# Rebuilding the entry of a feed-forward stage: operand tiles one by one, first weights ahead, two rooms for scaled rows

## The chip, the cores and the metric

The kernel runs on one core of a Trainium2 chip. The metric is the device time of one execution in microseconds (us), the median of several runs. One profiled execution of the kernel before is read beside them.

## What is computed

The program is one residual block on 1024 tokens of width 1024: a mixing stage (retention and forgetting attention), a cross attention, and a gated feed-forward. The change touches the entry of the last one:

```python
# reference, cut; h is (1, 1024, 1024), w_gate and w_up (1024, 2816), w_down (2816, 1024)
h = h + memory_cross_attention(rmsnorm(h, g_xattn), mem, ...)    # ends with  o @ w_xo
hn = rmsnorm(h, g_ffn)
h = h + (jax.nn.silu(hn @ w_gate) * (hn @ w_up)) @ w_down
```

All values are float32. Every matmul operand is cut in two parts (`hi`, a rounded copy made by ScalarE, and `lo`, the rest, made by VectorE), and a product of operands is three matmuls: hi·hi, hi·lo and lo·hi.

## The kernel before

**Stages.** `whole` (L1414) runs the mixing stage, `kv_main`, `wout_main`, `xattn_main`, `xo_main`, `hidden_main` and `down_main` in this order. The token rows go in eight tiles of 128 rows (t = 0 to 7), the 2816 hidden units in 22 blocks of 128 (f).

**Who sets the order.** Only TensorE's order is written out by hand. The stages are generators; the planner `Driver` (L93 on) takes a step of the first thread in its list that is ready, and otherwise a step of the main line. A step yields its estimated TensorE time in ns and a delay, which is stretched by `slow` (1.8 here). `take_tp` (L148 with `HOLD` 1.5) holds back transposes while both rooms of the PSUM tag `tp` are counted as taken. The orders of ScalarE, VectorE, GpSimd and SyncE come from the framework's list scheduler, which follows the program's order where nothing speaks against it. Every engine then runs its own queue strictly in order, and an instruction whose wait isn't over holds up all that stands behind it.

**Memory.** A tile belongs to a tag of a pool and the tag has `bufs` rooms. `raws` (L191) has three rooms of 4 KB under the tag `raw`. `wA` (L210) has five pairs `whi`, `wlo`, `big` (L213) eight rooms `b0` to `b7`, and `mx` (L860) the rooms `b8` to `b11`, `xs` (one row tile) and `gbc` (a broadcast gain). These three pools carry the weights and rows of the projection `w_xo` and belong to the stack `LW`. On the other side lie the residual rows `h` (stack `HP`, four tiles of two row tiles each) and `xr` (stack `R12`). Where a pool is closed and another opened on its bytes, a tile waits only for the users of older tiles on its own bytes.

**The way into the feed-forward.** `xo_main` (L1093) runs `out_proj` (L826): for each row tile two products of 24 matmuls with `w_xo`, VectorE adds them to `h[t]` (L838), and `f_norm(t)` (L1100) is spawned. `f_norm` waits until the row tile before it is done (`f_done`), scales the row into the single room `xs` (`norm`, L307 on: ScalarE squares at L310, a short chain of small operations, VectorE multiplies at L312), stores `h[t]` to DRAM, and after a delay transposes it on TensorE (L175) into `xr`. For t of 4 and more VectorE then makes four combinations of the quarters (L1125 to L1128). The 2x2 product of the tokens' two halves of rows and two halves of columns runs as seven block products (P1, P2, Q5, P6, P7, Q3, Q4), each of 12 matmuls per f.

`hidden_main` (L1174) begins as soon as four row tiles are done: for the first `AHEAD` = 3 blocks f it runs P1 and P2, whose weights (`load_gate`, L1155) are loaded through `raws` and lie in `b0` to `b5`. Then, with all eight row tiles done, `LW` is closed, a pool `ffn_x` is opened for the other five operands, and ScalarE and VectorE cut all five in two parts, first the columns 0 to 383 of all five, then 384 to 511 (L1250, L1251). After that `weights_of` (L1272) makes the weights of the products (sums `t13`, `t2`, `t4` of the four loaded blocks, then hi and lo), in the order Q5(0), P6(0), Q3(0), P7(0), Q5(1), Q4(0), ... `down_main` (L1307) follows.

Of the kernel before, what the change touches and what calls it, by code (L numbers as in the profile page):

```python
# [19 lines left out]
P = 128  # L20
D = 1024
T = 1024
NT = T // P
# [130 lines left out]
def trace(tc, a, out):  # L154
    nc = tc.nc
    ctx = ExitStack()
    drv = Driver()
# [51 lines left out]
    LW = ExitStack()  # L209
# [668 lines left out]
    def fox_end():  # L878
        yield lambda: fox_left[0] == 0 and hn_free[0] == NT
        FX.close()  # L880
        hp = pool("h", 1, side="right", stack=HP)
        pairs = [hp.tile([P, 2, D], F32, name=f"h{t}") for t in range(NT // 2)]
        st["h"] = [pairs[t // 2][:, t % 2] for t in range(NT)]
        st["h01"] = pairs[0].rearrange("p a (b c) -> p (a b) c", c=512)

    def kv_main():
# [206 lines left out]
    def xo_main():  # L1093
        w = st.pop("w_xo")
        h = st["h"]
        gff = gbc("gff")
        bcast(gff, a["g_ffn"])
        f_done = st["f_done"] = [0]

        def f_norm(t):  # L1100
            yield lambda: f_done[0] >= t
            xs = xs_tile("xs")
            norm(h[t], gff, xs)
            pol.dma_start(h_dram[t], h[t])
            yield 0.0, 4500.0
            cols = slice((t % 4) * P, (t % 4 + 1) * P)
            yield lambda: "xr" in st
            for b in range(2):
                yield from take_tp(2200)
                tp = ps_tp()  # L1110
                for j in range(4):
                    flip(tp[:, j, :], xs[:, (4 * b + j) * P:(4 * b + j + 1) * P])
                with prio(P_TP):
                    act.copy(st["xr"][t // 4][:, 4 * b:4 * b + 4, cols], tp)
                    if t < 4:
                        hi, lo = st["x1"][b][:, :4, cols], st["x1"][b][:, 4:, cols]
# [12 lines left out]
            f_done[0] += 1  # L1129
            yield 0.0, 2000.0  # L1130

        def opened():

            yield lambda: all(n == NX for n in o2_done)
            XA.close()
            xrp = pool("xr", 1, side="right", stack=R12)
            st["x1"] = [half(i, [P, 8, 512], "x1") for i in range(2)]
            st["xr"] = [xrp.tile([P, KC, 512], F32, name=f"xr{i}") for i in range(2)]

        drv.spawn(opened())  # L1140
        yield from out_proj(*st.pop("nxt_o2"), w, lambda t: None, lambda t: drv.spawn(f_norm(t)), first_gates)


# [16 lines left out]
    def first_gates():  # L1160
        st["gates"] = [load_gate(f) for f in range(AHEAD)]

    def into(q, terms, first):

        n = len(terms)
        for k, (wh, wl, xh, xl) in enumerate(terms):
            mm.matmul(q, wh, xh, start=first and k == 0, stop=False, skip_group_check=True)  # L1167
            mm.matmul(q, wh, xl, start=False, stop=False, skip_group_check=True)  # L1168
            mm.matmul(q, wl, xh, start=False, stop=k == n - 1, skip_group_check=True)  # L1169
            yield 700.0, 0.0  # L1170

    W1, RR = ExitStack(), ExitStack()

    def hidden_main():  # L1174

        f_done = st["f_done"]
        x1, xr = st["x1"], st["xr"]
        A = {"P1": (x1[0][:, :4], x1[0][:, 4:]), "P2": (x1[1][:, :4], x1[1][:, 4:])}
        alpha, beta, gamma, p1, s1, u2, q5, at = ({} for _ in range(8))
        pp, wp = [None], [None]  # L1180

        def row(f):
            if f not in at:
                at[f] = pp[0].tile([P, T], F32, name="at", tag="at")
            return at[f]

        def step(f, what, w):

            xh, xl = A[what]
            terms = [(w[0][:, k], w[1][:, k], xh[:, k], xl[:, k]) for k in range(4)]  # L1190
            if what == "P1":
                alpha[f] = ps_s()
                yield from into(alpha[f], terms, True)
                ab = raws.tile([P, 2, 512], F32, name="p1", tag="raw") if f < AHEAD else pp[0].tile([P, 2, 512], F32, name="p1", tag="p1")
                p1[f], s1[f] = ab[:, 0, :], ab[:, 1, :]
                act.copy(p1[f], alpha[f])
            elif what == "P2":
# [5 lines left out]
            elif what == "Q5":  # L1203
                gamma[f] = ps_tp().rearrange("p a b -> p (a b)")
                yield from into(gamma[f], terms, True)
                q5[f] = pp[0].tile([P, 512], F32, name="q5", tag="q5")
                act.copy(q5[f], gamma[f])
                if f < AHEAD:
                    act.activation(s1[f], s1[f], AF.Silu)
            elif what == "P6":  # L1210
                yield from into(alpha[f], terms, False)
                u2[f] = pp[0].tile([P, 512], F32, name="u2", tag="u2")
                act.copy(u2[f], alpha[f])
            elif what == "P7":
                yield from into(alpha[f], terms, False)
                c = row(f)
                dve.tensor_tensor(c[:, 512:], q5.pop(f), alpha[f], ALU.subtract)
            elif what == "Q3":
                yield from into(gamma[f], terms, False)
                c = row(f)  # L1220
                dve.tensor_tensor(c[:, :512], gamma.pop(f), u2.pop(f), ALU.subtract)
                dve.tensor_tensor(c[:, :512], c[:, :512], s1.pop(f), ALU.mult)
            else:
                yield from into(alpha[f], terms, False)
                s2 = pp[0].tile([P, 512], F32, name="s2", tag="s2")
                act.activation(s2, alpha.pop(f), AF.Silu)
                c = at.pop(f)
                dve.tensor_tensor(c[:, 512:], c[:, 512:], s2, ALU.mult)
                for g, hs in enumerate(GROUPS):
                    for i, fs in enumerate(hs):  # L1230
                        if f in fs:
                            pol.dma_start(a_dram[g][i][fs.index(f)], c)


        yield lambda: f_done[0] >= 4
        for f in range(AHEAD):
            gh, gl = st["gates"][f]
            yield from step(f, "P1", (gh[:, :4], gl[:, :4]))
            yield from step(f, "P2", (gh[:, 4:], gl[:, 4:]))

        yield lambda: f_done[0] == NT
        LW.close()
        wp[0] = pool("ffn_x", 1, stack=W1)
        xs = {"Q5": st["h01"], "P6": xr[0][:, :4], "P7": xr[1][:, :4], "Q3": xr[0][:, 4:], "Q4": xr[1][:, 4:]}
        for what, x in xs.items():
            A[what] = [wp[0].tile([P, 4, 512], F32R, name=f"x{what}{i}") for i in range(2)]
        for cols in (slice(0, 384), slice(384, 512)):
            for what, x in xs.items():
                hi, lo = (y[:, :, cols] for y in A[what])
                act.copy(hi, x[:, :, cols])  # L1250
                dve.tensor_tensor(lo, x[:, :, cols], f32(hi), ALU.subtract)  # L1251
        R12.close()
        HP.close()
        ra = pool("ffn_a", 1, side="right", stack=RR)
        rr = pool("ffn_w", 1, side="right", stack=RR)
        pp[0] = pool("ffn_t", 1, stack=W1)
# [4 lines left out]
        seq.insert(0, (0, "Q5"))  # L1261
        for f in range(AHEAD, NF_):
            seq += [(f, p) for p in ("P1", "Q5", "P6", "P2", "P7", "Q3", "Q4") if (f, p) not in seq]
        raw, t13, t2 = {}, {}, {}

        def load_w(f):

            raw[f] = r = ra.tile([P, 4, 4, P], F32, name="raw_w", tag="raw_w", bufs=2)
            for b, (src, k) in enumerate((("w_gate", 0), ("w_up", 0), ("w_up", 1), ("w_gate", 1))):
                sp.dma_start(r[:, b], a[src][k * 512:(k + 1) * 512, f * P:(f + 1) * P].rearrange("(k p) c -> p k c", p=P))  # L1270

        def weights_of(f, what):  # L1272
            r = raw[f]
            if what == "Q5":
                t13[f] = ra.tile([P, 2, 4, P], F32, name="t13", tag="t13", bufs=1)
# [17 lines left out]
                load_w(f + 2)  # L1293
            return hi, lo

        load_w(0)
        load_w(1)
        made = []
        for n, (f, what) in enumerate(seq):
            while len(made) < min(n + RING - 2, len(seq)):  # L1300
# [6 lines left out]
    def down_main():  # L1307
        h = {}
        RR.close()
        W1.close()  # L1310
        halves_stack.close()
        dl = pool("down_l", 1)
        dr = [pool(f"down_r{i}", 1, side="right") for i in range(2)]
# [139 lines left out]
```

## Time and profile before

| | us |
|---|---|
| median of 3 runs (1605.29 to 1613.33) | 1608.91 |
| the profiled execution, as timed | 1609.22 |
| its span in the trace | 1607.5 |

TensorE (PE) is busy for 1552.7 us of the span, VectorE (DVE) for 995.0, ScalarE (ACT) for 751.8, GpSimd (POOL) for 155.2. PE is the matrix engine's matmul queue, SP the queue of SyncE, which here only issues DMAs. A row of a timeline gives start and duration in us, engine, line, operation, output and inputs, and in brackets the idle time before it with what ended that. Matmuls overlap: a row of 0.39 us follows its predecessor after 0.23 us.

### The profile page before, as it was taken

Reading aid. Unit: us, or ns where it says so; the run is one execution under the profiler, and the core shown is the slowest. Engines: PE = TensorE matmul, PEld = TensorE weight load, DVE = VectorE, ACT = ScalarE, POOL = GpSimd, SP = SyncE. Lnnn points to the kernel's source line nnn. Section 1 sums busy time; section 2 is a strip of 40 time slices with the busy share of each in tenths; the row PEclk is TensorE's granted clock in tenths of the full one; section 3 lists DMA queues with packets and bytes.
Section 4 is the critical chain, followed back from the end, with each engine's and each line's share of the span. In section 5 each row is a group of like instructions: output and inputs, shape, how many; then the busy total and the mean of one; then the engine's idle time right before and its main releaser. Section 6 shows DMA issues by size and latency. Waiting matters only on the chain.

```text
span 1607.5 us, 21839 instructions
## 1 busy us (share of the span) xinstructions
PE 1552.7 (97%) x7960; PEld 1311.5 (82%) x7960; DVE 995.0 (62%) x2050; ACT 751.8 (47%) x1621; POOL 155.2 (10%) x318
## 2 busy tenths in 40 slices
PE   7999999999999999999989969999999999899998
PEld 6997897898898878888878857888888888688887
DVE  6667657657668943455554567555555554599994
ACT  5457566557658841355554344333333333234231
POOL 0332222232232000000000000000000000000000
PEclk9999999999999999999999989999999999999999
DMA  7031121121133471200343404222222222571202
GB/s 227 6 89 47 35 64 47 35 61 49 35 103 100 137 239 53 79 1 33 104 140 105 119 27 121 89 79 79 79 80 79 79 79 85 217 273 61 96 0 106
DMA packets 142798, 142.15 MB, mean 88 GB/s; under 512 B 9049, under 2 KB 110681, under 8 KB 142178
## 3 DMA queue, kind: packets, MB, share of 16 engines
q1 hardware_dynamic: 138370, 125.02, 25.2%
q0 software_dynamic: 4320, 15.73, 2.5%
q8 instruction: 63, 1.03, 0.3%
q14 instruction: 45, 0.37, 0.1%
HBM read 112.38 MB, written 28.34 MB: 88 GB/s over the span
## 4 chain that ended last, share of the span: by engine, by line
PE 85%; DVE 5%; ACT 5%; DMA 2%; issue 2%; POOL 1%; SPq 0%; POOLq 0%; DVEq 0%; ACTq 0%
PE ps_mm L270 10%; PE ps_mm L271 10%; PE ps_mm L272 10%; PE ps_s L1167 7%; PE ps_s L1169 7%; PE ps_s L1168 7%; PE ps_tp L175 5%; PE ps_tp L1167 4%; PE ps_tp L1168 4%; PE ps_tp L1169 4%; PE ps_mm L1168 2%; PE ps_mm L1169 2%; PE ps_mm L1167 2%; PE ps_pv L696 1%; PE ps_s L270 1%
## 5 line engine op out<-in xcount | busy, mean ns | idle before, releaser
L270 PE MATMUL ps_mm<-w_hi,cv_hi 128*128 128x512 f32 x384 | 156.0, 406 | 6.3 <-ACT qsq L1081 3.3
L272 PE MATMUL ps_mm<-w_hi,cv_lo 128*128 128x512 f32 x384 | 152.3, 397 | 0.0
L271 PE MATMUL ps_mm<-w_lo,cv_hi 128*128 128x512 f32 x384 | 152.1, 396 | 0.0
L1332 ACT CAST op<-raw_d 128x2048 fp32r<-128x2048 f32 (+1 forms) x42 | 72.7, 1764 | 126.5 <-issue 50.8
L1290 ACT CAST w_hi<-t 128x512 fp32r<-128x512 f32 x88 | 54.2, 621 | 160.2 <-PE ps_tp L1168 71.8
L240 DVE TENSOR_TENSOR w_lo<-raw,w_hi 128x1024 fp32r<-128x1024 f32 (+2 forms) x75 | 88.2, 1181 | 29.4 <-ACT w_hi L239 28.1
L239 ACT CAST w_hi<-raw 128x1024 fp32r<-128x1024 f32 (+2 forms) x75 | 74.9, 1003 | 58.1 <-PE ps_mm L272 39.5
L1291 DVE TENSOR_TENSOR w_lo<-t,w_hi 128x512 fp32r<-128x512 f32 x88 | 60.3, 687 | 65.8 <-ACT w_hi L1290 65.8
L270 PE MATMUL ps_mm<-w_hi,hn_last 128*128 128x384 f32 (+2 forms) x256 | 96.7, 378 | 1.0 <-DVE t L291 1.0
L270 PE MATMUL ps_mm<-w_hi,hn_hi 128*128 128x384 f32 (+2 forms) x256 | 96.2, 376 | 0.1
L1333 DVE TENSOR_TENSOR op<-raw_d,op 128x2048 fp32r<-128x2048 f32 (+1 forms) x42 | 87.3, 2109 | 8.1 <-ACT op L1332 8.1
L271 PE MATMUL ps_mm<-w_lo,hn_hi 128*128 128x384 f32 (+2 forms) x256 | 91.0, 356 | 0.0
L270 PEld LDWEIGHTS ps_mm<-w_hi,cv_hi 128*128 128x128 f32 x384 | 73.1, 190 | 21.8 <-ACT qsq L1081 3.8
L272 PE MATMUL ps_mm<-w_hi,hn_lo 128*128 128x384 f32 (+2 forms) x256 | 90.8, 355 | 0.0
L272 PE MATMUL ps_mm<-w_hi,hn_last 128*128 128x384 f32 (+2 forms) x256 | 90.4, 353 | 0.0
L271 PE MATMUL ps_mm<-w_lo,hn_last 128*128 128x384 f32 (+2 forms) x256 | 90.1, 352 | 0.0
L272 PEld LDWEIGHTS ps_mm<-w_hi,cv_lo 128*128 128x128 f32 x384 | 73.1, 190 | 17.0
L271 PEld LDWEIGHTS ps_mm<-w_lo,cv_hi 128*128 128x128 f32 x384 | 73.3, 191 | 14.7
L1167 PE MATMUL ps_tp<-xQ,w_hi 128*128 128x512 f32 x176 | 70.8, 402 | 14.0 <-ACT w_hi L1290 14.0
L1290 ACT CAST w_hi<-raw_w 128x512 fp32r<-128x512 f32 x60 | 37.2, 621 | 89.5 <-PE ps_s L1168 85.6
L1168 PE MATMUL ps_tp<-xQ,w_hi 128*128 128x512 f32 x176 | 70.9, 403 | 0.0
L1169 PE MATMUL ps_tp<-xQ,w_lo 128*128 128x512 f32 x176 | 70.7, 402 | 0.0
(378 smaller groups left out, 4255.5 us busy)
## 6 DMA issues: line engine op xcount, KB each, us to landing
raw_w<-w_gate SPq DMA_DIRECT2D x44, 256.0 KB, 3.1
raw_w<-w_up SPq DMA_DIRECT2D x44, 256.0 KB, 4.3
a_dram<-at POOLq DMA_DIRECT2D x22, 512.0 KB, 2.9
raw<-w_in SPq DMA_DIRECT2D x32, 256.0 KB, 4.0
raw<-w_xkv SPq DMA_DIRECT2D x16, 512.0 KB, 3.8
of<-o_dram SPq DMA_DIRECT2D x16, 512.0 KB, 4.1
raw_d<-a_dram SPq DMA_DIRECT2D x8, 1024.0 KB, 5.3
raw_d<-w_down SPq DMA_DIRECT2D x8, 1024.0 KB, 6.0
```

Source lines behind the costliest of these rows:

```text
L175: flip = lambda o, x: mm.transpose(o, x, ident)
L239: act.copy(hi, raw)
L240: dve.tensor_tensor(lo, raw, f32(hi), ALU.subtract)
L270: mm.matmul(o, xh, wh, start=first, stop=False)
L271: mm.matmul(o, xh, wl, start=False, stop=False)
L272: mm.matmul(o, xl, wh, start=False, stop=last)
L1167: mm.matmul(q, wh, xh, start=first and k == 0, stop=False, skip_group_check=True)
L1168: mm.matmul(q, wh, xl, start=False, stop=False, skip_group_check=True)
L1169: mm.matmul(q, wl, xh, start=False, stop=k == n - 1, skip_group_check=True)
L1290: act.copy(hi, x)
L1332: act.copy(hi, x)
L1333: dve.tensor_tensor(lo, x, f32(hi), ALU.subtract)
```

## The change

- `f_norm(t)` may scale its row when row tile t-2 is done (before: t-1). Odd rows take a room of `raws` for the scaled row, even ones the room `xs`. It still transposes only when row tile t-1 is done. The delay ahead of the last row's transposes is 2600 in place of 4500.
- The weights of Q5(0), P6(0), Q3(0), P7(0) and Q4(0) are made apart. `first_sums` loads the four blocks of f = 0 into the rows 4 and 5 of `h` once six rows have been scaled, and makes the sums in `b6`, `b7`. `first_weight` cuts them into `b8`, `b9`, `b10`, `xs` and `gbc`.
- The five operands take rooms of the pools that are open: Q5 and P6 two pairs of `wA` each, Q3 one pair and `b0`, `b1`, P7 `b2` to `b5`, Q4 `b8` to `b11`.
- The parts are cut operand by operand, each in two halves by rows of the contraction. The columns 0 to 383 of Q5, P6 and Q3 are cut by a thread that starts after P2(0) and when seven row tiles are done; their columns 384 to 511 and all of P7 follow when the eighth is done, Q4 after the steps Q5(0), P6(0), Q3(0).
- The temporaries of the loop over f (`at`, `p1`, `q5`, `u2`, `s2`) take the rooms `xs`, `gbc` and the first sums' two tiles. `LW` is closed in `down_main`.

```diff
         def f_norm(t):
-            yield lambda: f_done[0] >= t
-            xs = xs_tile("xs")
+            yield lambda: f_done[0] >= t - 1
+            xs = raws.tile([P, D], F32, name="xs", tag="raw") if t % 2 else xs_tile("xs")
             norm(h[t], gff, xs)
             pol.dma_start(h_dram[t], h[t])
-            yield 0.0, 4500.0
+            st["normed"] += 1
+            yield 0.0, 4500.0 if t < NT - 1 else 2600.0
             cols = slice((t % 4) * P, (t % 4 + 1) * P)
-            yield lambda: "xr" in st
+            yield lambda: "xr" in st and f_done[0] >= t
...
+    def first_sums():
+        yield lambda: st["normed"] > 5
+        blocks = lambda x: x.rearrange("p (b k c) -> p b k c", b=x.shape[1] // 512, c=P)
+        r = blocks(st["pairs"][2].rearrange("p a d -> p (a d)"))
+        load_blocks(r, 0)
+        t13, t24 = (bt(6 + i, [P, 2, 4, P], "t_first").bitcast(F32) for i in range(2))
+        dve.tensor_tensor(t13, r[:, 0:2], r[:, 1:3], ALU.add)
+        dve.tensor_tensor(t24[:, 0], t13[:, 0], r[:, 2], ALU.add)
+        dve.tensor_tensor(t24[:, 1], t24[:, 0], r[:, 3], ALU.add)
+        st["first"] = {"Q5": t13[:, 0], "P6": t24[:, 0], "Q3": r[:, 2], "P7": t13[:, 1], "Q4": t24[:, 1]}
+        st["t_room"] = [x.rearrange("p a k c -> p (a k c)") for x in (t13, t24)]
+
+    def first_weight(what, o):
+        x = st["first"][what]
+        hi, lo = (o[:, i].rearrange("p (k c) -> p k c", c=P) for i in range(2))
+        act.copy(hi, x)
+        dve.tensor_tensor(lo, x, f32(hi), ALU.subtract)
+        return hi, lo
...
-                at[f] = pp[0].tile([P, T], F32, name="at", tag="at")
+                at[f] = st["mx"].tile([P, T], F32, name="at", tag="xs", bufs=1)
...
-        yield lambda: f_done[0] >= 4
+        def operand(what, a, b):
+            A[what] = [[x[:, k] for x in (a[i], b[i]) for k in range(2)] for i in range(2)]
+            parts_of[what] = a, b
+
+        def parts(what, c0, c1):
+            for i, (hi, lo) in enumerate(parts_of[what]):
+                x = xs[what][:, 2 * i:2 * i + 2, c0:c1]
+                act.copy(hi[:, :, c0:c1], x)
+                dve.tensor_tensor(lo[:, :, c0:c1], x, f32(hi[:, :, c0:c1]), ALU.subtract)
+
+        yield lambda: f_done[0] >= 4 and "first" in st
+        first = {(0, what): first_weight(what, b_w(8 + i)) for i, what in enumerate(("Q5", "P6", "Q3"))}
         for f in range(AHEAD):
             gh, gl = st["gates"][f]
             yield from step(f, "P1", (gh[:, :4], gl[:, :4]))
             yield from step(f, "P2", (gh[:, 4:], gl[:, 4:]))
-
-        yield lambda: f_done[0] == NT
-        LW.close()
-        wp[0] = pool("ffn_x", 1, stack=W1)
-        xs = {"Q5": st["h01"], "P6": xr[0][:, :4], "P7": xr[1][:, :4], "Q3": xr[0][:, 4:], "Q4": xr[1][:, 4:]}
-        for what, x in xs.items():
-            A[what] = [wp[0].tile([P, 4, 512], F32R, name=f"x{what}{i}") for i in range(2)]
-        for cols in (slice(0, 384), slice(384, 512)):
-            for what, x in xs.items():
-                hi, lo = (y[:, :, cols] for y in A[what])
-                act.copy(hi, x[:, :, cols])
-                dve.tensor_tensor(lo, x[:, :, cols], f32(hi), ALU.subtract)
+            if f == 0:
+                operand("Q5", pair(), pair())
+                operand("P6", pair(), pair())
+                operand("Q3", pair(), [wide(0), wide(1)])
+
+                def ahead():
+                    yield lambda: f_done[0] >= NT - 1
+                    for what in ("Q5", "P6", "Q3"):
+                        parts(what, 0, 384)
+
+                drv.spawn(ahead())
+        yield lambda: f_done[0] == NT and st["normed"] == NT
+        for what in ("Q5", "P6", "Q3"):
+            parts(what, 384, 512)
+        first[0, "P7"] = first_weight("P7", st["mx"].tile([P, 2, 512], F32R, name="w_first", tag="xs", bufs=1))
+        first[0, "Q4"] = first_weight("Q4", st["mx"].tile([P, 2, 512], F32R, name="w_first", tag="gbc", bufs=1))
+        operand("P7", [wide(2), wide(3)], [wide(4), wide(5)])
+        parts("P7", 0, 512)
+        for what in ("Q5", "P6", "Q3"):
+            yield from step(0, what, first[0, what])
+        operand("Q4", [wide(8), wide(9)], [wide(10), wide(11)])
+        parts("Q4", 0, 512)
         R12.close()
         HP.close()
...
-        load_w(0)
         load_w(1)
+        load_w(2)
...
     def down_main():
         RR.close()
-        W1.close()
+        LW.close()
```

## Rows read from the trace of the kernel before

**Rows 1.** Waits over the whole span: engine, tile, line; total us, times, longest.

```profile
PE ps_tp L1167 <- ACT w_hi L1290: 14.0, 1, 14.0
```

**Rows 2.** Windows: stretch; PE, PEld, DVE, ACT, POOL busy (count); granted clock, DMA share, GB/s.

```profile
931.70:950.40 18.70, 18.69 (x89) 15.06 (x88) 9.05 (x16) 9.96 (x16) 0.53 (x1) 1.00 0.07 29
950.40:964.40 14.00, 0.00 (x0) 0.00 (x0) 13.87 (x13) 8.45 (x11) 0.00 (x0) 0.61 0.00 0
964.40:970.60 6.20, 6.17 (x15) 4.77 (x16) 6.12 (x10) 3.45 (x7) 0.00 (x0) 0.50 0.38 111
970.60:985.00 14.40, 14.40 (x63) 11.60 (x62) 12.78 (x20) 6.74 (x13) 0.00 (x0) 1.00 0.48 137
```

**Rows 3.** Timeline of PE at the entry.

```profile
917.71 1.04 PE L175 MATMUL ps_tp<-ident,xs 128*128 128x128 f32 x8
...
931.76 0.39 PE L1167 MATMUL ps_s<-x,w_hi 128*128 128x512 f32 x1
...
935.26 1.04 PE L175 MATMUL ps_tp<-ident,xs 128*128 128x128 f32 x8
...
944.49 1.04 PE L175 MATMUL ps_tp<-ident,xs 128*128 128x128 f32 x8
...
964.43 0.79 PE L1167 MATMUL ps_tp<-xQ,w_hi 128*128 128x512 f32 x1 [14.04 <-ACT w_hi L1290]
```

**Rows 4.** Timeline of DVE at the entry.

```profile
916.94 2.59 DVE L240 TENSOR_TENSOR w_lo<-raw,w_hi 128x1024 fp32r<-128x1024 f32 x2 [1.78 <-ACT w_hi L239]
...
940.71 1.29 DVE L312 SCALAR_TENSOR_TENSOR xs<-h,r,gff 128x1024 f32<-128x1024 f32 x1
...
946.41 0.69 DVE L1125 TENSOR_TENSOR h<-xr 128x512 f32<-128x512 f32 x1 [1.66 <-ACT xr L1114]
...
948.59 0.69 DVE L1128 TENSOR_TENSOR xr<-xr 128x512 f32<-128x512 f32 x1
950.50 0.69 DVE L1200 TENSOR_TENSOR p<-ps_mm,p 128x512 f32<-128x512 f32 x1 [1.22 <-PE ps_mm L1169]
951.11 1.75 DVE L1251 TENSOR_TENSOR xQ<-h,xQ 128x1536 fp32r<-128x1536 f32 x1
...
961.25 1.29 DVE L1251 TENSOR_TENSOR xQ<-xr,xQ 128x512 fp32r<-128x512 f32 x2
962.46 1.22 DVE L1276 TENSOR_TENSOR t<-raw_w 128x1024 f32<-128x1024 f32 x1
```

**Rows 5.** Timeline of ACT at the entry.

```profile
883.90 1.05 ACT L817 CAST cv_hi<-of 128x1024 fp32r<-128x1024 f32 x1 [2.01 <-PE ps_mm L271]
...
936.85 1.08 ACT L310 ACTIVATE xs<-h 128x1024 f32<-128x1024 f32 x1
...
938.97 1.28 ACT L1209 ACT_TABLE_LOAD   x1
940.26 0.63 ACT L1209 ACTIVATE p<-p 128x512 f32<-128x512 f32 x1
...
948.14 1.48 ACT L1250 CAST xQ<-h 128x1536 fp32r<-128x1536 f32 x1
```

**Rows 6.** Timeline of SP's DMA issues through `raws`, 870 to 900.

```profile
870.66 0.98 SPq L815 DMA_DIRECT2D of<-o_dram  x2
875.43 23.12 SPq L1157 DMA_DIRECT2D raw<-w_gate  x3
```

**Rows 7.** The page's DMA issues: count, KB each, median us from issue to landing.

```profile
of<-o_dram SPq DMA_DIRECT2D x16, 512.0 KB, 4.1
```

**Rows 8.** Timeline of PE behind two short waits elsewhere.

```profile
376.37 0.59 PE L175 MATMUL ps_tp<-ident,s_sb 128*128 128x128 f32 x3 [1.86 <-DVE kst L762]
...
1402.02 0.50 PE L1168 MATMUL ps_mm<-op,op 128*128 128x512 f32 x1 [1.33 <-DVE op L1333]
```

**Rows 9.** Window behind the first of them, columns as in rows 2.

```profile
376.40:382.00 5.60, 5.60 (x22) 4.60 (x23) 5.41 (x21) 4.93 (x14) 0.64 (x3) 0.70 0.32 94
```

**Rows 10.** Timeline of PE at the start of `down_main`.

```profile
1387.04 0.80 PE L1167 MATMUL ps_s<-op,op 128*128 128x512 f32 x1 [3.48 <-ACT op L1332]
```

More of the change, by code (lines that the diff above doesn't have):

```diff
@@ L883, in fox_end @@
         st["h"] = [pairs[t // 2][:, t % 2] for t in range(NT)]
+        st["pairs"] = pairs
         st["h01"] = pairs[0].rearrange("p a (b c) -> p (a b) c", c=512)
@@ L1138, in opened @@
             st["xr"] = [xrp.tile([P, KC, 512], F32, name=f"xr{i}") for i in range(2)]
+        st["normed"] = 0
         drv.spawn(opened())
+        drv.spawn(first_sums())
         yield from out_proj(*st.pop("nxt_o2"), w, lambda t: None, lambda t: drv.spawn(f_norm(t)), first_gates)
@@ L1161, in first_gates, with load_blocks @@
         st["gates"] = [load_gate(f) for f in range(AHEAD)]
+    def load_blocks(r, f):
+        for b, (src, k) in enumerate((("w_gate", 0), ("w_up", 0), ("w_up", 1), ("w_gate", 1))):
+            sp.dma_start(r[:, b], a[src][k * 512:(k + 1) * 512, f * P:(f + 1) * P].rearrange("(k p) c -> p k c", p=P))
+    def first_sums():
[15 more added lines that the diff above has]
+        return hi, lo
     def into(q, terms, first):
@@ L1170, in into @@
             yield 700.0, 0.0
-    W1, RR = ExitStack(), ExitStack()
+    RR = ExitStack()
     def hidden_main():
@@ L1177, in hidden_main @@
         x1, xr = st["x1"], st["xr"]
-        A = {"P1": (x1[0][:, :4], x1[0][:, 4:]), "P2": (x1[1][:, :4], x1[1][:, 4:])}
+        both = lambda x: [[x[:, 4 * i + k] for k in range(4)] for i in range(2)]
+        A = {"P1": both(x1[0]), "P2": both(x1[1])}
         alpha, beta, gamma, p1, s1, u2, q5, at = ({} for _ in range(8))
-        pp, wp = [None], [None]
         def row(f):
             if f not in at:
-                at[f] = pp[0].tile([P, T], F32, name="at", tag="at")
+                at[f] = st["mx"].tile([P, T], F32, name="at", tag="xs", bufs=1)
             return at[f]
@@ L1189, in step @@
             xh, xl = A[what]
-            terms = [(w[0][:, k], w[1][:, k], xh[:, k], xl[:, k]) for k in range(4)]
+            terms = [(w[0][:, k], w[1][:, k], xh[k], xl[k]) for k in range(4)]
             if what == "P1":
@@ L1193, in step @@
                 yield from into(alpha[f], terms, True)
-                ab = raws.tile([P, 2, 512], F32, name="p1", tag="raw") if f < AHEAD else pp[0].tile([P, 2, 512], F32, name="p1", tag="p1")
+                ab = raws.tile([P, 2, 512], F32, name="p1", tag="raw") if f < AHEAD else st["mx"].tile([P, 2, 512], F32, name="p1", tag="gbc", bufs=1)
                 p1[f], s1[f] = ab[:, 0, :], ab[:, 1, :]
@@ L1205, in step @@
                 yield from into(gamma[f], terms, True)
-                q5[f] = pp[0].tile([P, 512], F32, name="q5", tag="q5")
+                q5[f] = st["t_room"][0][:, :512]
                 act.copy(q5[f], gamma[f])
@@ L1211, in step @@
                 yield from into(alpha[f], terms, False)
-                u2[f] = pp[0].tile([P, 512], F32, name="u2", tag="u2")
+                u2[f] = st["t_room"][0][:, 512:]
                 act.copy(u2[f], alpha[f])
@@ L1224, in step @@
                 yield from into(alpha[f], terms, False)
-                s2 = pp[0].tile([P, 512], F32, name="s2", tag="s2")
+                s2 = st["t_room"][1][:, :512]
                 act.activation(s2, alpha.pop(f), AF.Silu)
@@ L1232, in step @@
                             pol.dma_start(a_dram[g][i][fs.index(f)], c)
-        yield lambda: f_done[0] >= 4
+        xs = {"Q5": st["h01"], "P6": xr[0][:, :4], "Q3": xr[0][:, 4:], "P7": xr[1][:, :4], "Q4": xr[1][:, 4:]}
+        wide = lambda i: bt(i, [P, 2, 512], "x_part")
+        pair = lambda: [wA.tile([P, 2, 512], F32R, name=f"x_{n}", tag=f"w{n}") for n in ("hi", "lo")]
+        def operand(what, a, b):
[6 more added lines that the diff above has]
+                dve.tensor_tensor(lo[:, :, c0:c1], x, f32(hi[:, :, c0:c1]), ALU.subtract)
+        parts_of = {}
+        b_w = lambda i: bt(i, [P, 2, 4, P], "w_first").rearrange("p a k c -> p a (k c)")
+        yield lambda: f_done[0] >= 4 and "first" in st
+        first = {(0, what): first_weight(what, b_w(8 + i)) for i, what in enumerate(("Q5", "P6", "Q3"))}
         for f in range(AHEAD):
@@ L1255, in hidden_main @@
         rr = pool("ffn_w", 1, side="right", stack=RR)
-        pp[0] = pool("ffn_t", 1, stack=W1)
         seq = []
@@ L1260, in hidden_main @@
             seq += [(f, "P6"), (f, "Q3"), (f, "P7"), (f + 1, "Q5" if f + 1 < AHEAD else "P1"), (f, "Q4")]
-        seq.insert(0, (0, "Q5"))
+        seq = seq[2:]
         for f in range(AHEAD, NF_):
@@ L1266, in load_w @@
         def load_w(f):
-            raw[f] = r = ra.tile([P, 4, 4, P], F32, name="raw_w", tag="raw_w", bufs=2)
-            for b, (src, k) in enumerate((("w_gate", 0), ("w_up", 0), ("w_up", 1), ("w_gate", 1))):
-                sp.dma_start(r[:, b], a[src][k * 512:(k + 1) * 512, f * P:(f + 1) * P].rearrange("(k p) c -> p k c", p=P))
+            raw[f] = ra.tile([P, 4, 4, P], F32, name="raw_w", tag="raw_w", bufs=2)
+            load_blocks(raw[f], f)
         def weights_of(f, what):
+            if (f, what) in first:
+                return first[f, what]
             r = raw[f]
```

## The prediction

> **What bounds the kernel now.** Read the list of waits over the whole span first: TensorE's longest wait by far is one of 14.0 us, at line 1167, the first product after P1 and P2 [rows 1]. Then the windows around it: from 950.4 to 964.4 TensorE does nothing while VectorE is busy for 13.87 of 14.00 us, and in the 6.2 us behind it the granted clock is 0.50, the lower of the two levels (1.2 GHz) [rows 2]. There 15 matmuls take 6.2 us; at the 14.40/63 = 0.229 us of the next window they take 3.4, so the clock costs 2.8 us more. The place is worth 14.0 + 2.8 = 16.8 us, which is the ceiling of what this change can give.
>
> The timelines say of what the wait consists. The last product with w_xo ends where P1 begins, at 931.76, but the square of row 7 starts only at 936.85, since the one room for scaled rows is held until row 6 is transposed at 935.26; row 7 is transposed at 944.49 [rows 3, 5]. Its four combinations end at 949.28, VectorE stands until the add behind P2(2) at 950.50, and from 951.11 to 962.54 cuts all five operands (two passes over five); then come the sum for the first weight (1.22) and its cast, and TensorE starts at 964.43 [rows 3, 4]. All of this is VectorE's queue; TensorE's supply of P1 and P2 ended at 964.43 - 14.04 = 950.39.
>
> **The change part by part** (times on the clock of this trace).
>
> *Row 7 earlier.* With a room of its own its square can follow the last add (a 512-column add takes 0.69): 932.5. From square to scaled row took 936.85 to 942.00 = 5.15, so it is ready by 937.7. The planner lets it transpose at 931.76 + 2.6 x 1.8 = 936.4, but row 6's transposes at 935.26 hold the tp rooms for 2.2 x 1.5 = 3.3, to 938.6, and the next break between groups of matmuls is near 939.0. So the transposes move 5.5 us ahead and the combinations end near 939.0 + 4.8 = 943.8. TensorE's work is the same, only in another place: 0.
>
> *Odd rows in the raw rooms.* Who shares them: the rows of the projection's input and the three gate loads. Two such rows are issued at 870.66 and the first is cut at 883.90, 13.2 later; a load lands in 4.1 [rows 5 to 7]. So 9 us of slack hide a room that comes late. Row 5's scaled row holds its room until its transposes at 917.71 [rows 3]; the third gate load, issued at 898.55 now [rows 6], then goes out near 918.8 and is cut by about 926 (4.1 + 1.3 + 1.3), for a P1(2) near 943. Cost 0; the price without cover is the second rival.
>
> *First weights ahead.* Removed from the path: 962.46 to 964.43, 1.97 us. Added beside other work: four DMAs on SP behind the gate loads (behind them stand only the loads for f = 1 and 2, due after 955), sums of 1.22 + 0.69 + 0.69 on VectorE, five hi casts of about 0.6 on ACT, five lo of 0.69. Three of the five have their rooms when the projection ends, at 931.76, and before row 7's multiply VectorE has room for their 2.1 us: it is busy for only 9.05 of the 18.70 us to 950.4 [rows 2]. Cost 0.
>
> *Operands one by one.* The five cuts cost VectorE 11.4 us between the last row and Q5 now [rows 4]; afterwards only Q5's must precede Q5(0). The 384 columns of three operands cost 3 x 1.75 = 5.3, from 943.8 to 949.1, with one add of 0.69 in between 949.8. The last columns are 2 x 0.34 per operand (half of 0.69). They stand in the program behind P2(2), whose add ran at 950.50, ahead of the cuts, in this trace. If it does again, Q5's first lo is there at 950.50 + 0.61 + 0.34 = 951.5, against TensorE's 950.4: a wait of 1.1. Below: 0, if the columns go ahead of the add (950.4). Above: if all of Q5's cut stands behind the add, 950.5 + 0.7 + 2.4 = 953.6, a wait of 3.2. I take 1.1, because the row at 950.50 shows the order. Q5(0), P6(0), Q3(0) then run from 951.5 in steps of 12 x 0.234 = 2.81 to 959.9; P6's and Q3's last columns (1.4), two lo weights (1.4) and P7's cut (2 x 1.22) are done by 957.
>
> *A new wait, at Q5(1).* Q4's second half takes b10 and b11, which hold Q3's first weight until Q3(0) ends at 959.9; cast 1.05 and lo 1.22 end at 962.2. The ring of the later weights lies on the bytes of xr, so Q5(1)'s lo weight has to wait for that, and behind it on VectorE's queue the lo of all later weights. Q5(1) starts at 962.7 and needs the lo at its third matmul, 963.2. Below: 962.2 + 0.69 = 962.9, no wait. Above: the sum (1.22), the cast (0.6) and three updates of `at` (which wait for P7's weight to leave `xs`, 2.1) all go first, 962.2 + 4.6 = 966.8, a wait of 3.6. The nearest row is the start at 964.43, 1.97 after the sum began behind the last cut [rows 3, 4]: 964.2, a wait of 1.0, which I take.
>
> *The clock behind short waits.* A wait of 1.86 was followed by 5.6 us at a mean of 0.70, so 3.4 us at the lower level, a loss of 1.7; behind one of 1.33 the first matmul took 0.50, not the 0.79 of the slow ones [rows 3, 8, 9]. So waits of 1.1 and 1.0 cost nothing more, and the upper ends cost 1.7 each: 4.9 and 5.3.
>
> *The rest.* The loop's temporaries had one room each and keep one: 0. `down_main` starts with a wait of 3.48 on a cast [rows 10], and its operands now lie on other old tiles: 0, with 2 us either way.
>
> **Sum.** 14.0 + 2.8 - 1.1 - 1.0 = 14.7. The profiled execution took 1609.2 us (span 1607.5 and 1.7 around it), so 1594.5; it lies 0.3 above the median, so 1594.2 for the median of the changed kernel. The forecast's own range is 1590 (no waits, 2 us off `down_main`) to 1597.5.
>
> **Rivals.**
>
> 1. *The queues' order leaves two waits.* TensorE's order is by hand, but VectorE's and ACT's follow the scheduler, and each of the two waits can reach its upper end: 1608.9 - 16.8 + 4.9 + 5.3 = 1602.3; a case between, 1597.5 to 1602. For it: VectorE stood 1.22 us for the add at 950.50 with cuts ready behind it (the cast of the first ended before 949.7) [rows 4, 5]. Against: the early columns stand in the program before P1(2).
>
> 2. *The raw rooms starve the rows; the slower end.* If the gate loads take all three rooms as they do now from 898.55 on, row 5's square waits for the first gate's cut, which ends near 918.2; the row is scaled at 923.4 where its transposes stand at 917.7: 5.7 and 1.7 for the clock, 7.4, so 1601.6 [rows 3, 4, 6]. Each load of the projection that in its turn waits for a scaled row and lies open costs 4.1 + 1.05 + 1.2 and the clock, 8.1. It decides from the second such stop on: 14.7 - 7.4 - 8.1 is below zero. With two loads open 1594.2 + 7.4 + 16.2 = 1618. Against: the 9 us of slack above, and that the gate loads went out at 875.43, after both rows of 870.66, though nothing but a room can have held them [rows 6]; rooms seem to be given in the program's order, which puts row 5 ahead of the gates.
>
> 3. *It doesn't do what it says.* The early cuts stay behind P2(2) and the three operands are cut before Q5(0) starts: 951.1 + 7.3 = 958.4, a wait of 8.0, with 1.7 and the upper end at Q5(1): 1608.9 - 16.8 + 15.0 = 1607.1. Against: no pool has to be closed for them now.
>
> 4. *Table loads.* The switch to Silu's table shows as 1.28 us at 938.97 with Silu right behind it at 940.26 [rows 5]. If Silu of f = 0 went ahead of row 7's Ln and Exp, two more loads would stand in row 7's way: 2.6 later, a first wait of 3.7 with 1.7 for the clock: 1598.5. Row 7's chain starts at 932.5 and P2(0) ends near 938.3, so it is unlikely. The Trainium skill, "ScalarE: Activation LUTs", section "What ACT_TABLE_LOAD costs", puts a switch at about 2.66 us, with a drain of 1.38 behind the load; by it the two would cost 5.3 and the time be near 1601. The row doesn't show the drain.
>
> **How the numbers follow.** Forecast 0.66, first rival 0.18, third 0.05, second with one stop 0.04 and with more 0.04, fourth 0.03. About 0.5% (8.0 us) is what a measurement of this kernel tells from no change, so faster means below 1600.9: 0.66 + 0.14 of the first rival + 0.03 = 0.83. Within: the rest of the first (0.04), one stop (0.04), the third (0.05) = 0.13. Slower: 0.04. The range from 1590 to 1602 holds the forecast, the first and fourth rival and one stop, and leaves out about 0.1.
>
> **What would show it.** Right: the wait of 14.0 gone from the list; row 7's transposes near 939; cuts of Q5, P6, Q3 between 941 and 950; Q5(0) near 951.5 at a granted clock of 1.00; a wait of about 1 at Q5(1). Wrong: a wait of TensorE for a scaled row near 918 (second rival); Q5(0) after 953 or a clock of 0.5 behind it (first, third); a longer wait at Q5(1), or idle time in the loop over f or at the start of `down_main` that isn't there now.

## The result, and the profile after

| | us |
|---|---|
| changed kernel, median of 6 runs (1591.84 to 1599.40) | 1594.94 |
| kernel before, 6 runs beside them (1604.06 to 1613.33) | 1606.36 |
| ratio, with its 95% interval | 0.9925 (0.9900 to 0.9949) |
| profiled execution, as timed (before: 1609.22) | 1593.67 |
| its span (before: 1607.5) | 1591.9 |

The changed kernel is faster by 0.75%. Its median of 1594.94 us lies 0.7 from the forecast of 1594.2. The profiled executions differ by 15.6 us, where 14.7 were forecast; the medians differ by 11.4, since the median of the kernel before is 1606.36 with six runs where it was 1608.91 with three. In a second series (5 runs against 10) the medians differ by 14.0, and the ratio was 0.9913 (0.9897 to 0.9929).

The list of TensorE's waits of the changed kernel, from 900 us to the end (columns as in [rows 1]; lines 1197 to 1199 are the products' matmuls, 1167 to 1169 before):

```profile
PE ps_s L1197 <- ACT op L1390: 3.5, 1, 3.5
PE ps_mm L1197 <- ACT op L1390: 2.5, 1, 2.5
PE ps_mm L1198 <- DVE op L1391: 1.6, 1, 1.6
PE ps_s L1198 <- DVE op L1391: 1.6, 1, 1.6
PE ps_tp L1199 <- DVE w_lo L1349: 0.9, 1, 0.9
PE ps_s L1197 <- DVE at L1247: 0.4, 1, 0.4
```

The 14.0 us are gone. Two small waits at the entry are new (the last two rows), and the first four belong to the start of `down_main`. There the second, the third and the fourth have grown, as the same list of the kernel before shows; more of them below.

```profile
PE ps_mm L1168 <- DVE op L1333: 1.3, 1, 1.3
PE ps_s L1168 <- DVE op L1333: 1.3, 1, 1.3
PE ps_mm L1167 <- ACT op L1332: 0.6, 1, 0.6
```

The windows of the changed kernel, columns as in [rows 2], each set as far behind the start of P1 as those of before:

```profile
929.80:948.50 18.70, 18.70 (x90) 15.39 (x90) 16.60 (x28) 16.82 (x31) 0.53 (x1) 1.00 0.34 85
948.50:962.50 14.00, 13.07 (x57) 10.30 (x56) 11.73 (x17) 6.85 (x10) 0.00 (x0) 1.00 0.00 1
962.50:968.70 6.20, 5.79 (x25) 4.42 (x24) 6.17 (x10) 4.17 (x8) 0.00 (x0) 1.00 0.60 169
968.70:983.10 14.40, 14.40 (x63) 11.63 (x62) 12.52 (x19) 5.42 (x10) 0.56 (x2) 1.00 0.35 110
```

The second window held no matmul before and now holds 57, at a granted clock of 1.00 throughout. VectorE's work moved one window ahead: 9.05 us of 18.70 were busy there before, now 16.60. How it is queued, in VectorE's timeline of the changed kernel (line 1277 is the low part of an operand's cut, 1230 the add behind P2, 1349 a weight's low part):

```profile
938.12 0.95 DVE L1277 TENSOR_TENSOR x_lo<-h,x_hi 128x768 fp32r<-128x768 f32 x1
...
946.08 0.95 DVE L1277 TENSOR_TENSOR x_part<-xr,x_part 128x768 fp32r<-128x768 f32 x1
946.95 0.68 DVE L1230 TENSOR_TENSOR p<-ps_mm,p 128x512 f32<-128x512 f32 x1
947.55 0.75 DVE L1277 TENSOR_TENSOR x_lo<-h,x_hi 128x256 fp32r<-128x256 f32 x2
948.22 0.42 DVE L1277 TENSOR_TENSOR x_lo<-xr,x_hi 128x256 fp32r<-128x256 f32 x1
948.63 0.69 DVE L1230 TENSOR_TENSOR p<-ps_mm,p 128x512 f32<-128x512 f32 x1
...
957.99 1.23 DVE L1277 TENSOR_TENSOR x_part<-xr,x_part 128x1024 fp32r<-128x1024 f32 x1 [1.80 <-ACT x_part L1276]
959.65 0.69 DVE L1251 TENSOR_TENSOR at<-ps_tp,t_first 128x512 f32<-128x512 f32 x1 [0.44 <-PE ps_s L1199]
960.26 0.68 DVE L1349 TENSOR_TENSOR w_lo<-t,w_hi 128x512 fp32r<-128x512 f32 x1
```

Q5's last columns (947.55) are cut ahead of the add behind P2(2) (948.63); before, every cut stood behind that add [rows 4]. TensorE in the changed kernel:

```profile
929.87 0.39 PE L1197 MATMUL ps_s<-x,w_hi 128*128 128x512 f32 x1
...
937.03 1.04 PE L175 MATMUL ps_tp<-ident,xs 128*128 128x128 f32 x8
...
948.36 0.39 PE L1197 MATMUL ps_tp<-x_hi,w_first 128*128 128x512 f32 x1
...
961.00 0.50 PE L1199 MATMUL ps_tp<-x_hi,w_lo 128*128 128x512 f32 x1 [0.93 <-DVE w_lo L1349]
...
964.00 0.50 PE L1197 MATMUL ps_s<-x_part,w_first 128*128 128x512 f32 x1 [0.41 <-DVE at L1247]
...
966.86 0.40 PE L1197 MATMUL ps_s<-x_hi,w_hi 128*128 128x512 f32 x1
...
1367.15 0.50 PE L1197 MATMUL ps_s<-op,op 128*128 128x512 f32 x1 [3.48 <-ACT op L1390]
```

Q5(0) starts at 948.36 with no wait. The row of P6(1) in the kernel before:

```profile
984.18 0.40 PE L1167 MATMUL ps_s<-xP,w_hi 128*128 128x512 f32 x1
```

From such rows the span divides into four stages: up to P1's first matmul; the entry, up to the first matmul of P6(1), the 145th matmul of these products (966.86 here, 984.18 before); the loop, up to the first matmul of `down_main`; and the rest.

| stage | before | changed | difference |
|---|---|---|---|
| to P1 | 931.76 | 929.87 | -1.9 |
| entry | 52.42 | 36.99 | -15.4 |
| loop | 402.86 | 400.29 | -2.6 |
| down projection | 220.46 | 224.75 | +4.3 |

The first row lies within the scatter: three profiles with the changed kernel's order gave 929.66 to 931.17, all fourteen of this study 925.8 to 932.3. Entry and loop come back to within 0.1 us wherever their order is the same, the down projection to within 1.7, so the experiments are read by stages rather than by totals, which scatter by up to 11 us among runs of one kernel.

### The profile page after: what moved, and what is told of

Its sections match the earlier page's. It is cut to its first block, busy times and chain, and to the rows that moved or that the text cites. A ratio compares the mean times of both kernels' runs of the same rounds, so it can differ in the third digit from the quotient of the medians.

```text
span 1591.9 us, 21842 instructions
## 1 busy us (share of the span) xinstructions
PE 1547.6 (97%) x7960; PEld 1308.2 (82%) x7960; DVE 994.5 (62%) x2056; ACT 752.6 (47%) x1627; POOL 155.3 (10%) x318
## 4 chain that ended last, share of the span: by engine, by line
issue 49%; PE 39%; DVE 4%; ACT 4%; DMA 2%; POOL 2%; SPq 0%; POOLq 0%; DVEq 0%; ACTq 0%
PE ps_mm L270 5%; PE ps_mm L271 5%; PE ps_mm L272 5%; PE ps_tp L175 3%; PE ps_s L1199 2%; PE ps_s L1197 2%; PE ps_s L1198 2%; PE ps_pv L696 1%; PE ps_mm L1198 1%; PE ps_mm L1199 1%; PE ps_mm L1197 1%; PE ps_tp L1199 1%; PE ps_tp L1197 1%; PE ps_tp L1198 1%; PE ps_pv L695 1%
## 5 line engine op out<-in xcount | busy, mean ns | idle before, releaser
L1199 PE MATMUL ps_s<-x_part,w_lo 128*128 128x512 f32 x168 | 66.3, 395 | 0.0
L1197 PE MATMUL ps_s<-x_part,w_hi 128*128 128x512 f32 x168 | 66.3, 395 | 0.0
L1198 PE MATMUL ps_s<-x_part,w_hi 128*128 128x512 f32 x168 | 66.2, 394 | 0.0
```

## The experiments

### What carries the gain: the rows, the weights, the early cuts, or the order

Each run takes one or two things from the changed kernel, or adds one to the kernel before. In the expectations the *queue theory* is that the first Q5 waits for VectorE's queue, that is for what stands in it ahead of Q5's operand and weight; the *row theory* is that it waits for row 7.

**Rows alone**, on the kernel before:

```diff
-            yield lambda: f_done[0] >= t
-            xs = xs_tile("xs")
+            yield lambda: f_done[0] >= t - 1
+            xs = raws.tile([P, D], F32, name="xs", tag="raw") if t % 2 else xs_tile("xs")
...
```

> The kernel before with the two rooms for scaled rows alone (every odd row in a tile of the raw weights' pool, the norm one row earlier); operands, pools and first weights as before. Queue theory (mine): the cuts of the operands cannot start before the last product of the projection has left its pools, and then stand behind its add on VectorE, so an earlier row 7 gives nothing: TensorE's idle time at the first Q5 stays 13 to 14 us and the time 1605 to 1607 us. Row theory (rival): the cuts follow row 7, whose transposes come 5.6 us earlier; the idle time falls to about 8.4 us and the time to about 1600 us. Starvation (rival, slower): the third gate block loads late, a stop at its product, over 1608 us.

Measured: 1.0003 (0.9989 to 1.0017) of before (1609.02 us, beside 1608.45 for the kernel before). Row 7 is transposed at 939.44, 7.16 us behind P1 instead of 12.73, and TensorE waits as long as ever:

```profile
939.44 1.03 PE L175 MATMUL ps_tp<-ident,xs 128*128 128x128 f32 x8
...
964.98 0.80 PE L1167 MATMUL ps_tp<-xQ,w_hi 128*128 128x512 f32 x1 [14.04 <-ACT w_hi L1290]
```

So an earlier row 7 alone gives nothing, and no product waits for a gate load.

**One room for rows again**, in the changed kernel (the same edit backwards):

> The changed kernel with one room for scaled rows again (norm of a row only after the row before it is done, wait of 4500 for the last). Row 7's transposes come 12.7 us after the first product of the projection instead of 7.2. Queue theory: the columns of rows 4 to 6 are cut meanwhile and only the 128 columns of row 7 follow, so the first Q5 waits 0 to 1 us; time 1595 to 1596 us. Row theory: the second room carries the gain, the first Q5 waits about 5.6 us and the time is about 1600.5 us.

Measured: 0.9910 (0.9892 to 0.9929) of before, 1594.32 us. Row 7 is transposed 12.74 us behind P1, and the entry takes 37.04 us, against 36.99: no wait at Q5(0).

**The early cuts taken out**, in the changed kernel:

```diff
-                drv.spawn(ahead())
...
-            parts(what, 384, 512)
+            parts(what, 0, 512)
```

> The changed kernel without the early cuts of 384 columns: each operand is cut whole, one after the other, from the end of row 7 on. Queue theory: between row 7's end (about 943.5 us on the changed kernel's clock) and the first Q5 (948.5) there is room for Q5's two cuts of 1.23 us, and then one operand's cuts (2.46 us) take less than one product (2.8 us), so the loss is 0 to 0.6 us; time 1595 to 1596 us. Rival (the early columns empty the queue): the six cuts of 0.87 us, 5.2 us, come back ahead of the first Q5; time 1600 us.

Measured: 0.9920 (0.9905 to 0.9935), 1595.35 us, entry 37.00 us. Taken out alone, they cost nothing.

**Both taken out at once**:

> The changed kernel with one room for scaled rows and without the early cuts, both covers taken away at once; first weights ahead and operands one by one stay. Queue theory: row 7's sums end about 947.4 us and Q5's two cuts run between them, so the first Q5 waits 0.5 to 2 us; time 1595.5 to 1597.5 us. Rival (the two covers together carry the gain): 5.6 us of row 7 and 5.2 us of cuts come back, 8 to 11 us of idle time, time 1604 us or more.

Measured: 0.9939 (0.9918 to 0.9961), 1596.29 us; entry 40.29 us, so 3.3 more. Q5(0) still doesn't wait, against my expectation; the delay appears at Q5(1), whose weight's two parts come later:

```profile
957.37 0.50 PE L1197 MATMUL ps_tp<-x_hi,w_hi 128*128 128x512 f32 x1 [1.50 <-ACT w_hi L1348]
...
959.07 0.50 PE L1199 MATMUL ps_tp<-x_hi,w_lo 128*128 128x512 f32 x1 [0.97 <-DVE w_lo L1349]
```

Those are 1.1 us more than 0.93 + 0.41; most of the rest is the clock, 0.77 in the 4.7 us behind 957.3 and 0.84 in the 4 us after. So the second room and the early cuts stand in for each other.

**The first weights late**: their sums and cuts, the load staying early, are tied behind Q5's last cut.

```diff
...
             parts(what, 384, 512)
+            if what == "Q5":
+                with tc.issue_after(st["cut"]):
+                    sums()
+                    first.update({(0, x): first_weight(x, b_w(8 + i)) for i, x in enumerate(("Q5", "P6", "Q3"))})
```

> The changed kernel with the sums and cuts of the first three weights held behind Q5's last cut on VectorE (their load stays early). Queue theory: the chain of sum 1.22, add 0.60, three steps of 0.60 and the cut 0.68 us now stands ahead of Q5's third matmul; the first Q5 waits about 3.8 us (2 to 5.5), time 1597 to 1600 us. Rival: the first weights' chain is hidden behind the projection's last products whatever its place, 0 us, time 1595 us.

Measured: 0.9933 (0.9917 to 0.9950), 1597.93 us; entry 41.58, so 4.6 more. The list of waits shows the high and the low part of Q5's weight (lines are one further down in this kernel):

```profile
PE ps_tp L1198 <- ACT w_first L1190: 1.4, 1, 1.4
PE ps_tp L1200 <- DVE w_first L1191: 1.1, 1, 1.1
```

These 2.5 us and 1.6 of clock (0.68 over the 5 us behind 951) are 4.1 of the 4.6 that making these three weights ahead of Q5's last cut is worth. The weights of P7(0) and Q4(0) stayed as they were.

**Cuts behind the add, operands one by one**: as without the early cuts, and each cut of VectorE tied behind the add of P2(2).

```diff
+                with tc.issue_after(st["add"]): dve.tensor_tensor(lo[:, :, c0:c1], x, f32(hi[:, :, c0:c1]), ALU.subtract)
...
```

> The changed kernel without the early cuts, and every cut of VectorE held behind the add of the projection's last product, as in the kernel before; operands whole and one by one, first weights made ahead. Queue theory: the add ends about 949.3 us, Q5's first cut takes 1.23 us more, so the first Q5 waits about 2 us instead of 0; later cuts keep up (1.2 us a half operand against 1.36 us of matmuls); time 1597 us (1596 to 1598.5). Rival (standing behind the add is the whole cost): 9 to 12 us of idle time, time 1604 us or more.

Measured: 0.9949 (0.9935 to 0.9963), 1598.75 us; entry 41.59, 4.6 more, above my range by a little. The waits:

```profile
949.67 0.50 PE L1198 MATMUL ps_tp<-x_lo,w_first 128*128 128x512 f32 x1 [1.76 <-DVE x_lo L1277]
...
963.42 0.50 PE L1199 MATMUL ps_tp<-x_hi,w_lo 128*128 128x512 f32 x1 [2.09 <-DVE w_lo L1349]
```

The first is what I had worked out (2). What I had not counted is the second: VectorE does not make up the delay before Q5(1), and the clock takes 1.7 (0.66 over the 5 us from 963).

**Cuts behind the add, by columns**:

```diff
...
+        for c in (0, 384), (384, 512): [parts(what, *c) for what in ("Q5", "P6", "Q3", "P7")]
```

> As the run before, but the four operands Q5, P6, Q3 and P7 are cut by columns (384 of each, then 128 of each), the order of the kernel before. Queue theory: eight cuts of 0.87 us and two of 0.38 stand ahead of the first Q5, which waits about 8.1 us, and 2 to 3 us go to the lower clock after it; time 1604 to 1607 us, most of what the change won. Rival (the order of the cuts does not matter): about 2 us of idle time, time 1597 us.

Measured: 0.9988 (0.9977 to 0.9999), 1605.40 us; entry 46.99, 10.0 more: a wait of 7.91 us and 2.1 of clock (0.64 over the 5.8 us behind it). Two thirds of the gain at the entry are gone, by where the cuts stand alone.

```profile
956.77 0.79 PE L1198 MATMUL ps_tp<-x_lo,w_first 128*128 128x512 f32 x1 [7.91 <-DVE x_lo L1277]
```

**One by one, on the kernel before**:

```diff
-        for cols in (slice(0, 384), slice(384, 512)):
-            for what, x in xs.items():
+        for what, x in xs.items():
+            for cols in (slice(0, 384), slice(384, 512)):
```

> The kernel before with one edit: the operands are cut one by one (all columns of one, then of the next) instead of by columns; rooms, pools and first weights as before. Queue theory with the rooms: the first weight's sum still stands behind the last cut on VectorE, because its rooms come free only there, so nothing is won: idle time 12.5 to 14.5 us, time 1605 to 1608 us. Rival (the order of the cuts alone does it): Q5 starts after its own two cuts, idle time 4 to 5 us, time about 1597 us.

Measured: 1.0003 (0.9990 to 1.0016); entry 52.39 us against 52.42.

```profile
962.35 0.80 PE L1167 MATMUL ps_tp<-xQ,w_hi 128*128 128x512 f32 x1 [14.04 <-ACT w_hi L1290]
```

What ended the wait tells why: it is the weight, not the operand. Its sum still runs behind the last cut (from 960.37 on, as the cuts end). In the program the pools of the weights are opened on the bytes of `xr` and `h`, which are being cut; that this is what keeps the sum back is argued, and no run moved that room alone. What the runs do show is that the order is worth nothing here, and 5.4 us (46.99 less 41.59) where the first weights are made ahead.

### What took 4 us back in the down projection

**The changed kernel once more, and a priority that changed no order.** The second of these two runs (`with prio(60 if g == 0 else 0):` around the operands of Q5) left VectorE's order as it was, so its expectation, written for another order, was not put to the test; it serves as one more execution.

> The changed kernel as it is, once more, beside the next two runs. If the waits at the start of the down projection belong to the change's layout (theory), its second product waits again 2.4 to 3.7 us for ScalarE's cast and 1.6 us for VectorE's, against 0.4 to 0.9 and 1.3 us in the kernels built on the one before; time 1594 to 1596 us. If they are a whim of one execution (rival), they fall to the values of before and the time to about 1591 us.

> The changed kernel with one order put back in the down projection: the difference of the loaded block A22 stands ahead of the sum of the loaded block B12 on VectorE, as in the kernel before. Theory (the order of the queue makes the wait): VectorE goes on when A22 has landed, some 2 us earlier, the cuts start about 3 us earlier, the second product waits 0 to 0.9 and 1.1 to 1.6 us instead of 2.5 and 1.6, and little of it runs at the lower clock; time 1591 to 1593 us. Rival (the loads themselves land late, beside eight loads of rows of h): the wait stays above 2 us and the time at 1594 to 1596 us.

Measured: 0.9913 (0.9897 to 0.9929), 1595.09 us, and 0.9914 (0.9896 to 0.9932), 1594.12 us. The second product waits 2.7 + 1.6 and 3.1 + 1.6 us. It is no whim of one execution: from the first matmul of `down_main` to the end, it takes 224.5 to 226.1 us in the nine profiles with the changed kernel's layout and order, 220.2 to 220.6 in the three with the layout of before. Of the 4.3 us between the two first profiles, 2.5 are the three waits that have grown (by 1.9, 0.3 and 0.3), and 1.7 a stretch at the lower clock behind those of 2.5 and 1.6 of the second product; behind the two in the same place of the kernel before, 0.6 and 1.3, the clock is 1.00 (1399 to 1406). The window of the changed kernel, columns as in [rows 2]:

```profile
1385.00:1390.00 5.00, 5.00 (x15) 3.91 (x16) 5.00 (x4) 2.95 (x2) 0.00 (x0) 0.66 1.04 408
```

VectorE's timeline of the changed kernel (1401 subtracts a loaded block, 1400 adds one):

```profile
1369.11 1.75 DVE L1401 TENSOR_TENSOR raw_d<-raw_d 128x1536 f32<-128x1536 f32 x1
1376.37 1.76 DVE L1400 TENSOR_TENSOR raw_d<-raw_d 128x1536 f32<-128x1536 f32 x1 [5.52 <-DMA raw_d<-w_down]
1378.05 1.75 DVE L1401 TENSOR_TENSOR raw_d<-raw_d 128x1536 f32<-128x1536 f32 x1
```

The sum of B12 stands ahead of the difference of A22, whose load was issued before B12's and could have gone first. In the kernel before, that difference (line 1343 there) stands ahead of the sum (1342):

```profile
1394.61 1.76 DVE L1343 TENSOR_TENSOR raw_d<-raw_d 128x1536 f32<-128x1536 f32 x1 [0.96 <-DMA raw_d<-a_dram]
...
1396.88 1.75 DVE L1342 TENSOR_TENSOR raw_d<-raw_d 128x1536 f32<-128x1536 f32 x1
```

**That order put back**, alone:

```diff
-                sub(a21, a21, a22)
-                add(b11, b11, b12)
+                first = sub(a21, a21, a22).ins
+                with tc.issue_after(first): add(b11, b11, b12)
```

> The changed kernel with the sum of block B12 tied behind the difference of block A22 on VectorE in the down projection (the order of the kernel before), and nothing else; the run named e7 raised a priority only and left that order as it was. Theory: from its first matmul to the end of the span the down projection takes 221.6 us, as in the run with both orders, against 224.5 to 226.1 in every kernel of the changed layout so far; the two small waits at the entry, 0.93 and 0.41 us, stay; time 1591 to 1593 us. Rival (the 221.6 us of that run came with its earlier clock, not with the order): 224.5 us or more, time 1594 to 1596 us.

Measured: 0.9893 (0.9876 to 0.9910), 1590.07 us, a little under my range; the down projection takes 221.36 us, the entry 36.99 as in the changed kernel. The same engine in this kernel:

```profile
1368.89 1.75 DVE L1401 TENSOR_TENSOR raw_d<-raw_d 128x1536 f32<-128x1536 f32 x1
1373.22 1.76 DVE L1401 TENSOR_TENSOR raw_d<-raw_d 128x1536 f32<-128x1536 f32 x1 [2.58 <-DMA raw_d<-a_dram]
1376.20 1.76 DVE L1400 TENSOR_TENSOR raw_d<-raw_d 128x1536 f32<-128x1536 f32 x1 [1.22 <-DMA raw_d<-w_down]
```

B12 lands when it did, but A22's difference has been made meanwhile, and the cuts behind them start at 1377.88 instead of 1381.39. So the order gives back 3.4 of the 4.3 us; for the 0.9 that stay no run shows a cause.

**And the two small waits of the entry**: as the run before, with the low part of Q5(1)'s weight ahead of row 0's difference, and the difference that frees alpha's bank ahead of three low parts (`cut[0]` is that low part).

```diff
-                dve.tensor_tensor(c[:, 512:], q5.pop(f), alpha[f], ALU.subtract)
+                with prio(30 if f == 0 else 0), tc.issue_after(cut[0]) if f == 0 else ExitStack(): dve.tensor_tensor(c[:, 512:], q5.pop(f), alpha[f], ALU.subtract)
...
+                if later and len(made) == 2:
+                    with tc.issue_after(cut[0]): later.pop()()
...
```

> As the run before, and at the entry the low part of Q5(1)'s weight put ahead of row 0's difference on VectorE, and the difference that frees alpha's bank ahead of three more low parts. Theory: the two small waits of the loop's first products, 0.93 and 0.41 us, fall to 0 to 0.3 each, 0.8 to 1.3 us less than the run before; time 1590 to 1592 us. Rival (the low part waits for its high part, not for the queue): 0.9 us stays, time as the run before.

Measured: 0.9870 (0.9857 to 0.9883), 1587.55 us; entry 35.41 us, 1.58 less, with no wait of TensorE's in it; down projection 221.59. The time lies below my range of 1590 to 1592. This is the fastest of all, 0.5% below the changed kernel beside it (1595.09). Of the 7.8 us between its profiled execution and the second one of the changed kernel, 1.6 are the entry, 3.3 the down projection and 2.9 the scatter ahead of P1.

## Why the prediction was right, point by point

- **The place and its price.** The entry became 15.43 us shorter; the ceiling of 16.8 less the two waits that are there now (0.93 + 0.41) is 15.46. Stage and clock were sized rightly.
- **Row 7 earlier.** Forecast 939.0 - 931.76 = 7.24 us behind P1, measured 937.03 - 929.87 = 7.16. The step happened as told, but what I hung on it, cuts that can only then begin, is true only in company: alone it gave nothing, and taken away it cost nothing as long as the early cuts were there.
- **Odd rows in the raw rooms.** The third gate load went out 929.87 - 917.45 = 12.4 us ahead of P1, forecast 13.0. No product waits for a row or a gate in any of the runs: the second rival did not happen. (The 898.55 that I read for the kernel before is where its third issue ended; it began at 898.19, which changes nothing here.)

```profile
917.45 0.37 SPq L1161 DMA_DIRECT2D raw<-w_gate  x1
```

- **First weights ahead.** I took 1.97 us, the chain to the first matmul alone. Tied behind Q5's cut it cost 4.6 us: its low part, the other sums ahead of it and the clock count too. The place of the term was right, its size too small. In the kernel before, where the weight stands behind the last cut, the order of the cuts is worth nothing; I did not say that the one hangs on the other.
- **Operands one by one.** I took a wait of 1.1 at Q5(0) from the row of before, where the add stood ahead of the cuts; it was 0, my lower bound, since the scheduler put Q5's last columns ahead of the add. The upper bound (all of Q5's cut behind the add, 3.2) was tried: 1.76 there, and 1.2 more at Q5(1).
- **The new wait at Q5(1).** Forecast 1.0, measured 0.93, for the low part, as told. The reason was half right: the low part could start behind Q4's last cut at 959.22, but row 0's difference went first, and waited 0.44 for TensorE with the low part behind it. Put ahead, it leaves no wait. The 0.41 at Q4(0) was in no term.
- **The clock.** Forecast unharmed, measured 1.00 in all four windows. In four runs with the changed layout it fell at the entry, behind waits of 1.42 and 1.11, of 1.50 and 0.97, of 2.09 and of 7.91 us, and cost 1.6 to 2.1 us, about the 1.7 that I had priced. Behind the 1.76 in the run with the cuts behind the add, one by one, it stayed at 1.00 (949.67 to 955): a wait of that length did not always cost what I took from the one of 1.86.
- **`down_main` at 0, with 2 us either way.** Mis-sized: +4.3. I had looked at where the operands lie, not at what a new layout does to the order that the scheduler gives VectorE. The loop, at 0, gave 2.6. The two cancel in part, and with the scatter ahead of P1 (-1.9 in these two profiles) they hide in a total that agrees. That the total came within 1 us is luck in part; the entry itself gave 15.4 us where 14.7 were forecast.
- **Table loads.** One load at the entry, as before, and Silu stands right behind it:

```profile
937.60 1.28 ACT L1239 ACT_TABLE_LOAD   x1
938.89 0.63 ACT L1239 ACTIVATE p<-p 128x512 f32<-128x512 f32 x1
```

Of the 2.66 us that the Trainium skill ("ScalarE: Activation LUTs", "What ACT_TABLE_LOAD costs") gives for a switch, the load's 1.28 is seen in both kernels, the drain of 1.38 in neither: the next operation starts 0.01 us after the load.

So the queue theory holds for the entry, with its parts weighed: of the entry's 15.4 us, 10.0 go when the cuts stand behind the add and by columns, 4.6 when they stand behind it but one by one, and 4.6 when the weights are made late; the parts overlap and don't add up.

## What to carry to other kernels

When an engine's queue is the wait, ask for each item in it who needs it first, and what keeps it from going earlier. Here neither an earlier input nor a better order alone gave anything; with the weights made ahead, in rooms of their own, the order was worth 5.4 us. (The rooms alone were not tried.) A change of layout also reorders, through the scheduler, stages that it doesn't touch; compare two traces stage by stage, and when one that should be equal is not, look at the order of the queue ahead of its first wait. A forecast that agrees in total can still hide two errors of opposite sign.

## What the runs showed of the hardware that was not expected

- **Equal matmuls, another pace.** In the loop nothing waits, and the same 128x512 matmuls follow each other faster in the changed layout. The windows from 1000 to 1300 us, the kernel before first, then the changed one (columns as in [rows 2]):

```profile
1000.00:1300.00 300.00, 300.00 (x1283) 241.16 (x1281) 158.96 (x230) 105.81 (x183) 8.51 (x16) 1.00 0.27 85
```

```profile
1000.00:1300.00 300.00, 300.00 (x1291) 241.90 (x1290) 160.83 (x232) 107.02 (x185) 7.97 (x15) 1.00 0.26 83
```

  That is 0.2338 against 0.2324 us each, at a clock of 1.00 in both; over the loop it makes the 2.6 us, 402.86 in all three profiles of the old layout and 400.29 to 400.30 in the eleven of the new. The two groups differ in the place of the operands and in the rooms of the loop's temporaries; which of these sets the pace is open.
- **The same short waits, another clock.** At the start of `down_main`, waits of 0.64 and 1.33 us left the clock alone in the kernel before, and so did 0.86 and 1.33 in the run that cuts one by one on the kernel before (1.00, the first row below). With 0.87 and 1.33 in the run with both orders, the seven matmuls from 1379.58 on took 0.63 us each, where 0.39 is usual, and the clock was 0.57 (the second row). A wait's length alone did not tell.

```profile
1398.00:1405.00 7.00, 5.39 (x22) 4.24 (x23) 7.00 (x6) 3.19 (x3) 0.00 (x0) 1.00 1.05 391
```

```profile
1379.00:1383.00 4.00, 4.00 (x12) 3.12 (x12) 4.00 (x3) 2.60 (x2) 0.00 (x0) 0.57 1.05 391
```
